# Expert layers of a two-layer trunk: unit 6's first half-weights loaded beside unit 4's, register reads per unit, gate products inside the second up product

## The chip, the cores and the metric

The kernel runs on one core of a Trainium2 chip. The metric is the device time of one execution in microseconds, the median of the runs. Times inside an execution are microseconds from the start of its span. Bytes are given as the profile gives them.

## What is computed

The program is a two-layer decoder trunk over 256 tokens of width 1024, float32 throughout. Layer 0 mixes with a state-space and a short-convolution mixer, layer 1 with two kinds of block-sparse attention. Each is followed by a hierarchical mixture of experts, which is what matters here:

```python
def hier_moe(h, w_group, b_group, w_expert, b_expert, w_gate, w_up, w_down):
    ...
    gi = jnp.argmax(gl, axis=-1)                                  # one of 4 groups per token
    ...
    ev, ei = lax.top_k(jax.nn.softmax(el, axis=-1), EXPERT_TOPK)  # 2 of the group's 4 experts
    ...
    h1 = jnp.einsum('td,edf->tef', xt, w_gate)
    h3 = jnp.einsum('td,edf->tef', xt, w_up)
    act = jax.nn.silu(h1) * h3 * gate[..., None].astype(h1.dtype)
    y = jnp.einsum('tef,efd->td', act, w_down)
```

There are 16 experts of 256 hidden units. Each has a gate, an up and a down matrix of 1 MB; a layer reads all 48 of them.

## The kernel before, in words

`moe(l, out_of)` computes one expert layer. Tokens are routed on the chip. `places` writes one-hot tables `Pm` that pick each expert's tokens; `gather(g, c0, c1)` multiplies the tokens by them and gives `xg`, the gathered tokens of a pair of units, in two halves of four column blocks. Work is done in seven units: units 0 to 5 have two experts with 64 token places each, unit 6 has four experts with 32 places each. Experts 0 to 5 stand fixed in units 0 to 2; `arrange` sorts the other ten by load, and their numbers (`ids`) are read into registers of SyncE, which issues all weight transfers in program order.

For unit j: `loads(j)` issues the gate and up weights, `downs(j)` the down weights, `up(j)` multiplies the gathered tokens by gate and up (c = 0..7 outside, the experts inside), `act(j)` applies SiLU on ScalarE and the product with the gate value `gs` on VectorE, `turn(j, a)` transposes the result on TensorE with a copy `aT` on VectorE, `down(j, f)` multiplies by half f of the down weights, `split` (L210 to L212) breaks the result into two parts on ScalarE and VectorE, and `scatter(j, f)` adds it back to `h` through the turned one-hot tables `PT`, which `ptrans(g)` makes.

Weights lie in slabs of 1 MB. Ten of them are a ring (`slab()`), and four more (`spare_slabs`) hold unit 2's gate and up weights and later the first halves of unit 6's. An expert's gate and up weights fill two slabs; `load_half(l, e, m, s)` issues the two transfers of one of them, for c = 4m to 4m + 3. A transfer into a slab waits until the work that reads its old content is done, and everything behind it in SyncE's queue waits too. In the loop, unit j's step issues the weights of unit j + 2 and the down weights of unit j + 1.

`gates` computes gate products: 14 small matmuls over the tables `Pm` and the gate values `Gs` (from `gate_values`, VectorE) whose sums give `gs` and the scale `rsl`, which `act` needs. The overflow test reads `nmax` into a register of every engine and branches around `overflow`, which is not taken here. PSUM tiles come from tags with a fixed number of buffers: `tp` has two, used by `gates`, `ptrans`, `gather` and `turn`; `mm` has two, used by `up`.

Each engine executes its instructions in the order in which the program issues them; the order is written out by hand.

Of the kernel before, what the change touches and what calls it, by code (L numbers as in the profile page):

```python
# [21 lines left out]
P = 128  # L22
# [38 lines left out]
FIX = 6  # L61
# [4 lines left out]
def tile_trunk(ctx: ExitStack, tc: tile.TileContext, x, cst, sml, s5c, ev_w_in, ev_w_out, od_w_in, od_w_out,  # L66
               cw1k, cw1v, w_gate, w_up, w_down, out):
    nc = tc.nc
# [7 lines left out]
    def ps(tag, shape, dt=F32):  # L76
        return psum.tile(shape, dt, name=tag, tag=tag, bufs={"acc": 3, "mm": 2, "tp": 2, "o": 1}[tag])
# [15 lines left out]
    def cs(n):  # L93
        o, w = _CST[n]
        return C[:, o:o + w]
# [12 lines left out]
    def slab():  # L108
        return ring.tile([P, 2048], F32, name="slab")
# [35 lines left out]
    def expert(w, l, e):  # L145
        return w[l, e] if isinstance(e, int) else w[l, bass.ds(e, 1)].rearrange("o a b -> (o a) b")

    def load_expert(l, e, s=None):

        return [load_half(l, e, m, slab() if s is None else s[m]) for m in range(2)]  # L150

    def load_half(l, e, m, s):
        v = s.rearrange("p (k c n) -> p k c n", k=2, c=4)
        for k, w in enumerate((w_gate, w_up)):
            sy.dma_start(v[:, k], expert(w, l, e).rearrange("(p c) f -> p c f", c=8)[:, 4 * m:4 * m + 4])  # L155
        return v

    def load_down(l, es):

        out = []  # L160
        for e in es:
            s = slab().rearrange("p (c n) -> p c n", c=2)
            sy.dma_start(s, expert(w_down, l, e).rearrange("(p c) d -> p c d", c=2))
            out.append(s)
        return out
# [1072 lines left out]
    def moe(l, out_of):  # L1238
        with tc.tile_pool(name=f"moe{l}", bufs=1, reuse_waits="tile") as sp:
# [39 lines left out]
            for t in range(2):  # L1279
                p = ps("tp", [P, 20])  # L1280
# [32 lines left out]
            nd = 16 - FIX  # L1313
            sd, ids, Q = T("sd", (P, 2, nd)), T("ids", (P, nd), I32), T("Q", (P, nd, nd))
            slx, nmax = T("slx", (P, 2, 16)), T("nmax", (P, 1), I32)

            def places(a, b):

                n, w = b - a, 64 if a < 12 else 32
                o = 64 * a if a < 12 else 768 + 32 * (a - 12)  # L1320
                for t in range(2):
                    v = sl[:, t, a:b] if a < FIX else sd[:, t, a - FIX:b - FIX]
                    tt(Pm[:, t, o:o + n * w].rearrange("p (e s) -> p e s", e=n), v[:, :, None].to_broadcast([P, n, w]),
                       cs("iota")[:, None, 0:w].to_broadcast([P, n, w]), op=OP.is_equal)
# [67 lines left out]

            def gates():

                p = ps("tp", [P, 512])
                for j in range(7):
                    for t in range(2):
                        pe.matmul(p[:, 34 * j:34 * j + 192], pair(t, j), Gs[:, t], start=(t == 0), stop=(t == 1))
                for k in range(2):
                    v = p[64 * k:64 * k + 64]  # L1400
                    d = bass.AP(tensor=v.tensor, offset=v.offset + k, ap=[v.ap[0], [36, 6], [16, 2]])
                    tr(gs[64 * k:64 * k + 64, 0:6, None], d, axis=AX.X, op=OP.add)
                for k in range(4):
                    v = p[32 * k:32 * k + 32]
                    d = bass.AP(tensor=v.tensor, offset=v.offset + 34 * 6 + 12 + k, ap=[v.ap[0], [1, 1], [16, 2]])
                    tr(gs[32 * k:32 * k + 32, 6:7, None], d, axis=AX.X, op=OP.add)
                d = bass.AP(tensor=p.tensor, offset=p.offset + 32, ap=[p.ap[0], [34, 7], [1, 2]])
                tr(rsl[:, :, None], d, axis=AX.X, op=OP.add)
                tt(gs, gs, rsl, op=OP.mult)
# [22 lines left out]
            def ptrans(g):  # L1432
                p = ps("tp", [P, 2, 2, P])
                n = 2 if g < 3 else 1
                for jj in range(n):
                    for t in range(2):
                        pe.transpose(p[:, jj, t], pair(t, 2 * g + jj).bitcast(F32), ident)  # L1437
                ac.activation(PT[:, 2 * g:2 * g + n], p[:, :n], AF.Copy)

            wgu, wd, pgu, ys = {}, {}, {}, {}  # L1440

            who = list(range(FIX))
            of = lambda j: who[2 * j:2 * j + 2] if j < 6 else who[12:]
            spare_slabs = lambda: [T(f"slab{i}", (P, 2048)) for i in range(4)]

            def loads(j):
                if j == 2:
                    x = spare_slabs()
                    wgu[j] = [load_expert(l, e, x[2 * k:2 * k + 2]) for k, e in enumerate(of(j))]
                elif j == 6:  # L1450

                    x = spare_slabs()
                    v = [load_half(l, e, m, x[k] if m == 0 else slab()) for m in range(2) for k, e in enumerate(of(j))]
                    wgu[j] = [[v[k], v[4 + k]] for k in range(4)]
                elif j < 7:
                    wgu[j] = [load_expert(l, e) for e in of(j)]

            def downs(j):
                wd[j] = load_down(l, of(j))

            def up(j):
                pgu[j] = p = ps("mm", [P, 2, 256])
                n = len(wgu[j])
                w = P // n
                for c in range(8):
                    for k in range(n):
                        o = P * (j % 2) + w * k
                        pe.matmul(p[w * k:w * k + w], xgs[j // 2][:, c, o:o + w], wgu[j][k][c // 4][:, :, c % 4],  # L1468
                                  start=(c == 0), stop=(c == 7), tile_position=(0, w * k))
# [51 lines left out]
            up(0)  # L1521
            arrange()
            gate_values()
            places(4, 6)
            places(6, 12)
            places(12, 16)
            gates()
            ptrans(0)
            cnt = nc.values_load(nmax[0:1, 0:1], min_val=0, max_val=288)
            with tc.If(cnt > 64):  # L1530
                overflow(sp, l, xT, slx, Gf, rs, T("xg", (P, 8, 256), bufs=2))
            a = act(0)
            for j in range(6):
                g = j // 2
                if j == 1:
                    who += [nc.values_load(ids[0:1, i:i + 1], engines=(mybir.EngineType.SP,), min_val=FIX, max_val=15)
                            for i in range(nd)]
                if j:
                    loads(j + 2)
                downs(j + 1)  # L1540
                up(j + 1)
                aT = turn(j, a)
                if j:
                    scatter(j - 1, 0)
                a = act(j + 1)
                more = j % 2 == 0
                if more:
                    gather(g + 1, 0, 4)
                down(j, 0)
                if j:  # L1550
                    scatter(j - 1, 1)
                down(j, 1)
                if more:
                    gather(g + 1, 4, 8)
                else:
                    ptrans(g + 1)
# [53 lines left out]
    moe(0, False)  # L1610
    odd()
    moe(1, True)


# [93 lines left out]
```

## Time and profile before

| | |
|---|---|
| median of 3 runs | 530.35 us (528.98 to 530.55) |
| the profiled execution | 529.48 us, its span 527.8 us |
| TensorE (PE) busy | 490.3 us, 93% |
| VectorE (DVE) busy | 293.4 us, 56% |
| ScalarE (ACT) busy | 212.9 us, 40% |
| transfers | 137.63 MB, mean 261 GB/s |

The first expert layer lies between about 119 and 247 us of the span, the second between about 395 and 524 us. Busy time is that of an engine's instructions; an engine that is busy for most of the span can still have short waits that set the end. A releaser (behind `<-`) is what ended an idle time.

### The profile page before, as it was taken

How to read it: one execution, taken by the hardware profiler on the slowest of the kernel's cores; microseconds unless marked ns; L12 is line 12 of the kernel's file. 1: busy time of each engine (PE TensorE's matmuls, PEld its weight loads, DVE VectorE, ACT ScalarE, POOL GpSimd, SP SyncE). 2: the span in 40 equal slices, each digit the busy share in tenths (PEclk: the TensorE clock that was granted, in tenths of full speed). 3: DMA queues.
4: the chain of work that ended last, by engine and by line, in shares of the span. 5: the costliest groups of instructions: out<-in, count | busy, mean ns of one | idle time of the engine just before them, and what ended most of it. 6: DMA issues, size and time to landing. Idle time of an engine off the chain costs nothing. (4 is left out here: it accounts for less than half of the span.)

```text
span 527.8 us, 9043 instructions
## 1 busy us (share of the span) xinstructions
PE 490.3 (93%) x3245; PEld 330.9 (63%) x3245; DVE 293.4 (56%) x682; ACT 212.9 (40%) x468; POOL 138.9 (26%) x292
## 2 busy tenths in 40 slices
PE   7998979998899999998899889989998899999995
PEld 5997979786354443544878778878785453443441
DVE  5876597656723323434654687977456623333432
ACT  4646623754131111214546777777563121111110
POOL 6899970001000000100355556651230000000000
PEclk9999997999999999999999999999999899999999
DMA  8949933357497899999959400440088595999992
GB/s 299 405 136 381 380 116 111 130 213 266 172 339 289 289 397 403 413 420 399 377 189 377 174 2 13 142 160 8 2 283 354 204 362 233 323 390 412 398 385 84
DMA packets 36591, 137.63 MB, mean 261 GB/s; under 512 B 4544, under 2 KB 8768, under 8 KB 31424
## 3 DMA queue, kind: packets, MB, share of 16 engines
q1 hardware_dynamic: 36544, 137.03, 68.5%
q8 instruction: 27, 0.44, 0.3%
q14 instruction: 20, 0.16, 0.1%
HBM read 135.70 MB, written 1.05 MB: 259 GB/s over the span
## 5 line engine op out<-in xcount | busy, mean ns | idle before, releaser
L1468 PE MATMUL mm<-slab,xg 128*64 128x512 f32 (+1 forms) x512 | 101.4, 595 | 1.6 <-DMA slab<-in_w_up_dram 1.0
L1468 PEld LDWEIGHTS mm<-slab,xg 128*64 128x64 f32 (+1 forms) x512 | 34.5, 130 | 58.3 <-issue 56.2
L1485 DVE COPY aT<-tp 128x256 f32<-128x256 f32 x14 | 6.0, 425 | 76.9 <-PE tp L1483 76.9
L212 DVE TENSOR_TENSOR w<-slab,w 128x1024 fp32r<-128x1024 f32 (+2 forms) x39 | 40.0, 1034 | 13.5 <-ACT w L211 12.3
L313 PE MATMUL mm<-xh,w 128*128 128x256 f32 x288 | 41.2, 293 | 3.8 <-DVE yb L372 3.3
L211 ACT ACTIVATE w<-slab 128x512 fp32r<-128x512 f32 (+2 forms) x57 | 43.3, 780 | 1.3 <-PE mm L837 0.9
L313 PEld LDWEIGHTS mm<-xh,w 128*128 128x128 f32 x288 | 38.1, 200 | 4.2 <-issue 4.2
L837 PE MATMUL mm<-w,xh 128*128 128x256 f32 x256 | 38.6, 293 | 0.2 <-ACT xh L242 0.2
L1474 ACT ACTIVATE si<-mm,rsl 128x256 f32<-128x256 f32 x14 | 6.7, 475 | 75.7 <-PE mm L1468 67.8
L837 PEld LDWEIGHTS mm<-w,xh 128*128 128x128 f32 x256 | 33.3, 189 | 1.2 <-ACT xh L242 0.9
L1497 PE MATMUL o<-slab,aT 128*64 128x512 f32 (+1 forms) x128 | 29.5, 604 | 2.9 <-DMA slab<-in_w_down_dram 2.9
L1509 DVE TENSOR_TENSOR h<-h,acc 128x512 f32<-128x512 f32 x44 | 28.2, 682 | 2.8 <-PE acc L1506 2.8
L212 DVE TENSOR_TENSOR ylp<-o,xlp 128x512 fp32r<-128x512 f32 x14 | 9.7, 692 | 34.4 <-ACT xlp L211 34.4
L1497 PE MATMUL acc<-slab,aT 128*64 128x512 f32 (+1 forms) x128 | 28.6, 600 | 0.0
L849 POOL MEMSET fl<- 128x2048 f32 x1 | 1.8, 1805 | 98.9 <-PE tp L1422 98.9
L212 POOL TENSOR_TENSOR w<-slab,w 128x512 fp32r<-128x512 f32 (+1 forms) x18 | 24.0, 1343 | 13.9 <-ACT w L211 9.5
L1428 ACT ACTIVATE xg<-tp,sml 128x256 f32<-128x256 f32 (+1 forms) x32 | 12.6, 444 | 36.0 <-PE tp L1422 36.0
L407 PE MATMUL acc<-w,yh 128*128 128x512 f32 x80 | 25.7, 400 | 0.0
L211 ACT ACTIVATE xlp<-o 128x512 fp32r<-128x512 f32 x14 | 8.4, 598 | 42.8 <-PE acc L1506 28.3
L1107 ACT ACTIVATE pr<-acc,mx 128x128 f32<-128x128 f32 (+1 forms) x56 | 22.9, 424 | 0.1
L398 DVE TENSOR_TENSOR w<-slab,w 128x512 fp32r<-128x512 f32 (+1 forms) x18 | 17.1, 963 | 10.4 <-ACT w L397 8.7
L1422 PEld LDWEIGHTS tp<-Pm,xhm 128*128 128x128 f32 x128 | 16.5, 189 | 9.7 <-issue 4.9
(436 smaller groups left out, 1004.0 us busy)
## 6 DMA issues: line engine op xcount, KB each, us to landing
slab<-in_w_gate_dram SPq DMA_DIRECT2D x64, 512.0 KB, 8.4
slab<-in_w_up_dram SPq DMA_DIRECT2D x64, 512.0 KB, 9.1
slab<-in_w_down_dram SPq DMA_DIRECT2D x32, 1024.0 KB, 10.4
slab<-in_ev_w_in_dram SPq DMA_DIRECT2D x8, 1024.0 KB, 13.9
slab<-in_od_w_in_dram SPq DMA_DIRECT2D x8, 1024.0 KB, 12.7
slab<-in_ev_w_out_dram SPq DMA_DIRECT2D x4, 1024.0 KB, 12.3
slab<-in_od_w_out_dram SPq DMA_DIRECT2D x4, 1024.0 KB, 8.8
slab<-in_ev_w_in_dram SPq DMA_DIRECT2D x4, 512.0 KB, 7.6
```

The costliest lines, as they stand in the source:

```text
L211: ac.activation(hi, src, AF.Copy)
L212: (eng or ve).tensor_tensor(lo, src, hi.bitcast(F32), op=OP.subtract)
L313: pe.matmul(p, a[:, c], b[:, c], start=(c == 0 and n == 0), stop=(c == 7 and n == 2))
L398: (po if s.done in s.pool else ve).tensor_tensor(wl, v[:, o:o + s.n], wh.bitcast(F32), op=OP.subtract)
L407: pe.matmul(acc[t, f], a[:, c, t * P:(t + 1) * P], b[:, f * 512:(f + 1) * 512], start=(first and m == 0), stop=(last and m == 2))
L837: pe.matmul(acc[i][t], a[:, c0 + k, t * P:(t + 1) * P], b[:, k], start=(c0 + k == 0 and m == 0 and (n > 256 or t == 0)), stop=(c0 + k == 7 ...
L1107: ac.activation(pr[:, q * nk:(q + 1) * nk], U[u]["s"][:, q * w:q * w + nk], AF.Exp, bias=U[u]["m"][:, q:q + 1], accum_out=su[:, q:q + 1])
L1422: pe.matmul(p[b][:, d], v[:, t, c], Pm[:, t, 256 * g:256 * g + n_], start=(n + d + t == 0), stop=(n + t == 2), skip_group_check=True)
L1428: ac.activation(xgs[g][:, c, :n_], p[b][:, d], AF.Copy, scale=w)
L1468: pe.matmul(p[w * k:w * k + w], xgs[j // 2][:, c, o:o + w], wgu[j][k][c // 4][:, :, c % 4], start=(c == 0), stop=(c == 7), tile_position=( ...
L1497: pe.matmul(py[v], aT[:, c, v], wd[j][k][:, c, f * 512:(f + 1) * 512], start=(c == 0), stop=(c == 1), tile_position=(0, w * k))
L1509: tt(v, v, q[t], op=OP.add)
```

## The change

In each expert layer, `up(1)` is cut into two halves and moved. Its first half (c = 0..3) now stands ahead of the gate products, its second half between `ptrans(0)` and the overflow test. `downs(1)` is issued ahead of the test. The first half of `gather(1)` moves ahead of `turn(0)`. `places(12, 16)` is called inside `gates`, at the same place in VectorE's order.

The register reads are no longer ten in a row: `of(j)` reads the registers of a unit when its weights are first asked for. The first halves of unit 6 (into the four spare slabs) are issued with unit 4, between the weights of its first and its second expert; unit 6's own step issues the second halves alone.

```diff
             def gates():
 
+                places(12, 16)
                 p = ps("tp", [P, 512])
...
-            who = list(range(FIX))
-            of = lambda j: who[2 * j:2 * j + 2] if j < 6 else who[12:]
+            who = {}
+
+            def of(j):
+
+                if j not in who:
+                    a, b = (2 * j, 2 * j + 2) if j < 6 else (12, 16)
+                    who[j] = [i if i < FIX else nc.values_load(ids[0:1, i - FIX:i - FIX + 1], min_val=FIX, max_val=15,
+                                                               engines=(mybir.EngineType.SP,)) for i in range(a, b)]
+                return who[j]
...
+                elif j == 4:
+
+                    wgu[j] = [load_expert(l, of(j)[0])]
+                    wgu[6] = [[load_half(l, e, 0, x)] for e, x in zip(of(6), spare_slabs())]
+                    wgu[j].append(load_expert(l, of(j)[1]))
                 elif j == 6:
-
-                    x = spare_slabs()
-                    v = [load_half(l, e, m, x[k] if m == 0 else slab()) for m in range(2) for k, e in enumerate(of(j))]
-                    wgu[j] = [[v[k], v[4 + k]] for k in range(4)]
+                    for k, e in enumerate(of(j)):
+                        wgu[j][k].append(load_half(l, e, 1, slab()))
...
-            def up(j):
-                pgu[j] = p = ps("mm", [P, 2, 256])
+            def up(j, c0=0, c1=8):
+                if c0 == 0:
+                    pgu[j] = ps("mm", [P, 2, 256])
+                p = pgu[j]
...
-                for c in range(8):
+                for c in range(c0, c1):
...
             gate_values()
+            up(1, 0, 4)
             places(4, 6)
             places(6, 12)
-            places(12, 16)
             gates()
             ptrans(0)
+            up(1, 4, 8)
+            downs(1)
             cnt = nc.values_load(nmax[0:1, 0:1], min_val=0, max_val=288)
...
             for j in range(6):
                 g = j // 2
-                if j == 1:
-                    who += [nc.values_load(ids[0:1, i:i + 1], engines=(mybir.EngineType.SP,), min_val=FIX, max_val=15)
-                            for i in range(nd)]
+                more = j % 2 == 0
                 if j:
                     loads(j + 2)
-                downs(j + 1)
-                up(j + 1)
+                    downs(j + 1)
+                    up(j + 1)
+                else:
+                    gather(1, 0, 4)
                 aT = turn(j, a)
...
-                more = j % 2 == 0
-                if more:
+                if j and more:
                     gather(g + 1, 0, 4)
```

TensorE's order from unit 0's up product (L1468 before, L1482 now) to unit 0's down product (L1497 before, L1511 now), the rows of the branch's untaken side left out. Before:

```order
L1468 MATMUL mm<-slab,xg 64x512 x16
L1398 MATMUL tp<-Gs,Pm 128x192 x14
L1437 MATMUL tp<-sml,Pm 128x128 x4
L1529 TENSOR_LOAD nmax
L1530 COMPARE_AND_BRANCH
...
L1468 MATMUL mm<-slab,xg 64x512 x16
L1483 MATMUL tp<-sml,act 128x128 x2
L1422 MATMUL tp<-Pm,xhm 128x256 x8
L1422 MATMUL tp<-Pm,xlm 128x256 x8
L1497 MATMUL o<-slab,aT 64x512 x4
```

Now:

```order
L1482 MATMUL mm<-slab,xg 64x512 x24
L1399 MATMUL tp<-Gs,Pm 128x192 x14
L1438 MATMUL tp<-sml,Pm 128x128 x4
L1482 MATMUL mm<-slab,xg 64x512 x8
L1545 TENSOR_LOAD nmax
L1546 COMPARE_AND_BRANCH
...
L1423 MATMUL tp<-Pm,xhm 128x256 x8
L1423 MATMUL tp<-Pm,xlm 128x256 x8
L1497 MATMUL tp<-sml,act 128x128 x2
L1511 MATMUL o<-slab,aT 64x512 x4
```

Eight of unit 1's sixteen up matmuls have moved ahead of the gate products and eight ahead of the branch, and the gather's first half stands ahead of the turn, not behind it.

SyncE's queue at unit 4 of layer 0; `slab_2110` to `slab_2113` are the four spare slabs, and in the ring's rows gate and up alternate. Before, unit 4's four slabs were followed by unit 3's down weights:

```order
L155 DMA slab<-in_w_gate_dram 128x1024
L155 ISA
L155 DMA slab<-in_w_up_dram 128x1024
L163 ISA
L163 DMA slab<-in_w_down_dram 128x2048
L163 ISA
L163 DMA slab<-in_w_down_dram 128x2048
```

Now, behind unit 4's first expert:

```order
L155 DMA slab<-in_w_up_dram 128x1024
L1449 TENSOR_LOAD ids
...
L155 DMA slab_2110<-in_w_gate_dram 128x1024
L155 ISA
L155 DMA slab_2110<-in_w_up_dram 128x1024
...
L155 DMA slab_2113<-in_w_gate_dram 128x1024
L155 ISA
L155 DMA slab_2113<-in_w_up_dram 128x1024
L155 ISA
L155 DMA slab<-in_w_gate_dram 128x1024
```

Four register reads and eight transfers of unit 6 now stand between unit 4's first and second expert.

## Rows read from the trace of the kernel before

**Rows 1.** The page: the span, and TensorE's busy time, share of the span and instructions.
```profile
span 527.8 us, 9043 instructions
PE 490.3 (93%) x3245; PEld 330.9 (63%) x3245; DVE 293.4 (56%) x682; ACT 212.9 (40%) x468; POOL 138.9 (26%) x292
```
**Rows 2.** The chain of work that ended last, in order of time: start, duration, what.
```profile
474.46 13.91 DMA slab<-in_w_up_dram
...
499.00 17.87 DMA slab<-in_w_down_dram
```
**Rows 3.** TensorE's timeline in layer 0, from unit 0's second gather half and up product to the start of unit 2's up product: start, duration, engine, line, operation, count, idle time before it and its releaser.
```profile
129.14 1.25 PE L1422 MATMUL tp<-Pm,xhm 128*128 128x256 f32 x8 [0.69 <-ACT xg L1428]
...
131.26 7.09 PE L1468 MATMUL mm<-slab,xg 128*64 128x512 f32 x32
140.47 2.37 PE L1398 MATMUL tp<-Gs,Pm 128*128 128x192 f32 x14 [2.13 <-DVE Gs L1388]
142.68 0.60 PE L1437 MATMUL tp<-sml,Pm 128*128 128x128 f32 x4
143.57 7.18 PE L1468 MATMUL mm<-slab,xg 128*64 128x512 f32 x32 [0.30 <-PEq L1530]
150.68 0.44 PE L1483 MATMUL tp<-sml,act 128*128 128x128 f32 x2
...
151.64 0.98 PE L1422 MATMUL tp<-Pm,xhm 128*128 128x256 f32 x6 [0.28 <-DVE aT L1485]
...
153.46 1.94 PE L1497 MATMUL o<-slab,aT 128*64 128x512 f32 x8
...
157.04 1.21 PE L1422 MATMUL tp<-Pm,xhm 128*128 128x256 f32 x8
...
159.12 7.09 PE L1468 MATMUL mm<-slab,xg 128*64 128x512 f32 x32
```
**Rows 4.** TensorE's timeline in layer 1: units 0 and 2's up products, the gate products, and the two waits in unit 6.
```profile
406.53 7.09 PE L1468 MATMUL mm<-slab,xg 128*64 128x512 f32 x32
415.74 3.15 PE L1398 MATMUL tp<-Gs,Pm 128*128 128x192 f32 x14 [2.12 <-DVE Gs L1388]
...
435.50 7.09 PE L1468 MATMUL mm<-slab,xg 128*64 128x512 f32 x32
...
502.14 3.59 PE L1468 MATMUL mm<-slab,xg 128*32 128x512 f32 x26 [0.69 <-DMA slab<-in_w_up_dram]
...
516.92 1.47 PE L1497 MATMUL o<-slab,aT 128*32 128x512 f32 x9 [1.43 <-DMA slab<-in_w_down_dram]
```
**Rows 5.** TensorE's timeline in layer 0: unit 3's up product and the turn behind it, unit 4's up product, and the two waits in unit 6.
```profile
172.88 7.09 PE L1468 MATMUL mm<-slab,xg 128*64 128x512 f32 x32
179.90 0.44 PE L1483 MATMUL tp<-sml,act 128*128 128x128 f32 x2
...
189.95 7.09 PE L1468 MATMUL mm<-slab,xg 128*64 128x512 f32 x32
...
225.36 3.59 PE L1468 MATMUL mm<-slab,xg 128*32 128x512 f32 x26 [0.31 <-DMA slab<-in_w_up_dram]
...
240.20 1.48 PE L1497 MATMUL o<-slab,aT 128*32 128x512 f32 x9 [1.44 <-DMA slab<-in_w_down_dram]
```
**Rows 6.** The timeline of SyncE's queue (SPq) in layer 0: the last transfer for unit 4's first expert, the first for its second, and the first for unit 6.
```profile
158.81 0.33 SPq L155 DMA_DIRECT2D slab<-in_w_up_dram  x1
172.38 0.33 SPq L155 DMA_DIRECT2D slab<-in_w_gate_dram  x1
...
194.73 0.33 SPq L155 DMA_DIRECT2D slab<-in_w_gate_dram  x1
```
**Rows 7.** Stretches of 5 us in layer 0: the stretch, its length, the engines' busy time and instructions, the granted clock, the share of the transfer engines, GB/s.
```profile
165.00:170.00 5.00, 5.00 (x23) 2.09 (x20) 2.11 (x4) 0.48 (x1) 0.00 (x0) 1.00 0.52 210
170.00:175.00 5.00, 5.00 (x25) 1.73 (x25) 2.57 (x4) 1.75 (x3) 0.00 (x0) 1.00 0.30 93
175.00:180.00 5.00, 5.00 (x25) 1.54 (x22) 0.00 (x0) 0.00 (x0) 0.00 (x0) 1.00 0.91 265
180.00:185.00 5.00, 5.00 (x31) 3.32 (x31) 2.98 (x6) 1.32 (x3) 0.00 (x0) 1.00 1.03 430
```
**Rows 8.** VectorE's timeline in layer 0: the last one-hot tables, and unit 0's activation.
```profile
140.74 1.42 DVE L1323 TENSOR_TENSOR Pm<-sd,cst 128x384 fp32r<-128x384 f32 x4
...
147.24 0.48 DVE L1476 SCALAR_TENSOR_TENSOR act<-mm,gs,si 128x256 f32<-128x256 f32 x1 [2.95 <-ACT si L1474]
```
**Rows 9.** ScalarE's timeline in layer 0: the table load ahead of unit 0's SiLU, and the two copies of one gather half.
```profile
145.44 1.28 ACT L1474 ACT_TABLE_LOAD   x1 [1.47 <-DVEq L1530]
...
153.34 0.84 ACT L1428 ACTIVATE xg<-tp,sml 128x256 f32<-128x256 f32 x2 [2.02 <-PE tp L1422]
```
**Rows 10.** The stretches of the gate products of layers 0 and 1, columns as in Rows 7.
```profile
140.50:143.00 2.50, 2.39 (x17) 2.09 (x18) 1.78 (x7) 0.00 (x0) 0.00 (x0) 1.00 1.01 423
415.00:420.00 5.00, 3.96 (x19) 3.60 (x19) 3.34 (x17) 0.28 (x1) 0.00 (x0) 0.66 0.68 281
```
**Rows 11.** The instructions of L1536, the register reads of both layers: duration in ns least, median, greatest, and the first and last start.
```profile
L1536 SPq TENSOR_LOAD <-ids x20: 261/267/282, 137.6 to 418.1; - x20
L1536 SPq FUSED_REGOPS  x20: 147/147/154, 137.9 to 418.4; - x20
```
**Rows 12.** The transfers of L163, the down weights, issued between 190 and 246 us.
```profile
DMA to landing us min/median/max: 8.0/13.1/17.0
```

## Prediction

> **What bounds the kernel now.** I read the page's totals first, then the chain of waits, then TensorE's timeline through both expert layers, and last the queue that issues the weight transfers. TensorE is busy for 93% of the span [rows 1], so a change pays only where it fills one of TensorE's waits or shortens its work. The chain that ended last [rows 2] runs from 474 us to 517 us almost wholly through weight transfers and only then back into matmuls: in the second expert layer the weights of the last units arrive too late.
>
> TensorE's timeline shows four kinds of wait in each expert layer. (a) Between the first up product and the gate products TensorE idles 2.13 us in layer 0 [rows 3] and 2.12 us in layer 1 [rows 4]: VectorE is still computing the gate values Gs. (b) After the overflow branch it idles 0.30 us, and after the first turn it idles until VectorE has copied aT; from the start of that turn to the next matmul behind the copy it is 151.64 - 150.68 = 0.96 us [rows 3]. (c) In unit 6's up product it waits for a second half of weights, 0.31 us [rows 5] and 0.69 us [rows 4]. (d) In unit 6's down product it waits 1.44 us [rows 5] and 1.43 us [rows 4].
>
> The cause of (c) and (d) stands in the transfer queue. After 158.81 us it issues nothing until 172.38 us: the next transfer goes into a slab that unit 1's down product still reads [rows 6]. The rate falls to 210, 93 and 265 GB/s in the three stretches from 165 to 180 us, and then runs at 430 [rows 7]. From 194.73 us [rows 6] unit 6's eight slabs and the last six down slabs are wanted at once, and unit 6 pays for the hole.
>
> **The change, part by part.** Layer 0 is worked out from the start of unit 0's up product to the start of unit 2's, which takes 159.12 - 131.26 = 27.86 us now [rows 3]. An unhindered up product of two experts takes 179.90 - 172.88 = 7.02 us from its start to the next work [rows 5], half of one 3.51. The new order costs, step by step:
>
> - up(0), 7.02: to 138.28.
> - first half of up(1), 3.51: to 141.79. Its weights were issued long before and its gathered tokens are the ones that up(0) reads, so it has nothing to wait for.
> - gate products. Gs is complete before VectorE starts its last one-hot tables at 140.74, and these end at 142.16 [rows 8]. So the wait of 2.13 is gone. The products cost 142.68 - 140.47 = 2.21 now [rows 3]; some of this may be waiting for the tables, but I keep all of it: to 144.00.
> - the turned one-hot tables, 0.60 [rows 3]: to 144.60.
> - second half of up(1), 3.51: to 148.11.
> - the branch. I take the 0.30 that it costs today [rows 3], since the engine still drains ahead of it: to 148.41.
> - first half of gather(1), 159.12 - 157.04 = 2.08 [rows 3]: to 150.49.
> - a new wait. The turn now needs a PSUM buffer that the gather's copies must first empty. The nearest row is the second gather half of unit 0's pair, which stands in the same position behind the first half, 0.69 [rows 3]: to 151.18. Bounds: nothing, and 0.84 more if both of ScalarE's copies come after the last matmul (they are two of the kind that took 0.84 together [rows 9]).
> - the turn with the wait for its copy, 0.96 as now [rows 3], which no gather work covers any more: to 152.14.
> - both halves of down(0), 157.04 - 153.46 = 3.58 [rows 3]: to 155.72.
> - second half of gather(1), 2.08: to 157.80.
>
> So unit 2 starts at 157.80 and not at 159.12: **1.3 us** in layer 0. Of the 2.13 us filled, 0.8 go back into the turn's two waits, since the gather that covered them has moved ahead.
>
> In layer 1 the same stretch takes 435.50 - 406.53 = 28.97 us [rows 4], 1.11 more than in layer 0. The work is the same; the granted clock was 0.66 in the stretch of its gate products, and 1.00 in layer 0's [rows 10], that is, part of it ran at 1.2 GHz instead of 2.4. The engine had waited 2.12 us just before. With matmuls in the place of that wait I expect the full clock, so the gain there is 1.3 + 1.1 = **2.4 us**. The Trainium skill, "TensorE: Matmul & The Clock Gate", Part 1, says that the array's clock is halved by inactivity and released by sustained activity; by that the 1.1 us go with the wait. The trace agrees in layer 1 and not in layer 0, where the same wait left the clock at 1.00.
>
> **The transfers.** The first halves of unit 6 go into the four spare slabs, which up(2) frees, half of them at its middle and the rest by its end, some 166 us [rows 3, 5]. They are four slabs of 1024 KB, 4.2 MB. The hole in [rows 7] has room for (410 - 210 + 410 - 93 + 410 - 265) GB/s x 5 us = 3.3 MB, with 410 GB/s for a full queue, a little under the 430 shown. So the work behind it comes 3.3 MB / 410 GB/s = 8 us earlier at the least. Unit 6's late slabs were 0.31 and 1.44 us late, and TensorE will ask 1.3 us earlier: 8 us covers 1.44 + 1.3 = 2.7. Both waits go: 0.31 + 1.44 = **1.75 us** in layer 0, 0.69 + 1.43 = **2.12 us** in layer 1. Bounds: nothing, and these sums. I take them whole, because the margin is 5 us.
>
> **What else moves, at nothing.** Ten register reads take their place one by one: each is a load of 0.27 and a register operation of 0.15 us [rows 11], some 0.5 with the gaps. Now only two stand ahead of unit 3's first weights, which therefore start some 4 us earlier; unit 3 does not wait for weights today, so this buys nothing by itself. The four reads of unit 6's registers, 2 us, fall into the queue's 13 us of waiting. Unit 1's down slabs are issued ahead of the branch, which only the transfer queue sees. The branch itself is passed later by TensorE alone. The chain from the gate products to the turn has to be watched: from the start of the turned tables at 142.68 to the end of unit 0's activation at 147.24 + 0.48 = 147.72 it is 5.04 us [rows 3, 8], with ScalarE's table load of 1.28 in it [rows 9]. From 144.00 this gives 149.04, and the turn asks at 151.18: 2.1 us in hand.
>
> **The sum.** 1.3 + 2.4 + 1.75 + 2.12 = 7.6 us. The profiled execution took 529.48 us, so 521.9; it stands 0.87 us below the median of 530.35, from which the same sum gives 522.8. I give **522.4**, between them. The stretches between the expert layers are bound by TensorE's order, and their weights come earlier too, so I let the gain of layer 0 pass through whole. About 0.3%, 1.6 us, is what a measurement here can tell from no change.
>
> **Rivals.**
> 1. The clock falls in both layers. Three waits of 0.3, 0.69 and about 0.5 us now stand within four microseconds. For it: layer 1 [rows 10]; against it: waits like these stand around gather(0) in layer 0 at a clock of 1.00. It costs the 1.11 us of layer 1 twice: 522.4 + 2.2 = 524.6. The Trainium skill, same page, "A second HAM failure mode", says that frequent short idling between groups of matmuls makes the clock swing; that speaks against this change, and by it this rival is the outcome.
> 2. The cover is too thin: unit 0's activation comes later than the turn by more than the 2.1 us in hand and the 1.3 us gained per layer are lost: 522.4 + 2.6 = 525.0. Against it: every link of the 5.04 us is a row, and none has the changed work in it.
> 3. The transfers do not gain: unit 6's first halves come early, but the down slabs, issued last, stay late. Then only 3.7 us remain: 526.3. For it: the queue is full from 180 us on [rows 7] and the down slabs need up to 17.0 us to land [rows 12]. Against it: 4.2 MB less stand ahead of them.
> 4. Slower: unit 4's second expert is now issued behind unit 6's first halves. It would be issued at 172.38 - 1.3 = 171 us [rows 6] and is wanted at 189.95 - 1.3 = 188.7 [rows 5]. If it lands later than 17.6 us after issue, every further microsecond delays TensorE, in both layers; from 22.4 us on (2 x 4.8 = 9.6 more) the kernel is slower than before. The longest landing shown is 17.0 [rows 12]; at 23 us it costs 2 x 5.4 = 10.8, and the time is 533. The Trainium skill, "DMA: Bandwidth & Descriptors", "Queues, rings and completion order", says that each transfer engine takes its descriptors in ring order, so that what is issued first is ahead; by it the eight early transfers stand ahead, as this rival has it, and no row shows the order on an engine. Against the rival: the hole nearly holds the 4.2 MB, and the 0.9 left over are 2 us.
> 5. No change that can be measured, because something in the layers between takes the gain back: about 530.
>
> **How the numbers follow.** The forecast has 0.72; rival 1 has 0.09, rival 2 0.06, rival 3 0.08, rival 4 0.02, rival 5 0.03. The forecast's own range is 520.2 (no new wait at the turn, 2 x 0.69 less, and 0.8 for half of the spread of the three runs) to 524.0 (0.84 more at the turn in one layer, and the same 0.8). With rivals 1 and 2 the range is 520.2 to 525.2, which leaves out 0.13. Faster by over 0.3%: forecast and rivals 1 to 3, 0.95; within 0.3%: 0.03; slower: 0.02.
>
> **What would show it.** In the changed profile: no idle time of TensorE ahead of the gate products; about 0.7 ahead of unit 0's turn and 0.5 ahead of unit 0's down product; the granted clock 1.00 through layer 1's gate products; some 26.5 us from up(0) to up(2) in both layers; no wait for a weight transfer in unit 6; a transfer rate above 380 GB/s from 160 to 180 us. A wait for weights ahead of unit 4's up product, or unit 6's waits unchanged, would prove me wrong.

## The result, and the profile after

The changed kernel takes 516.39 us (median of 4 runs, 514.40 to 516.89) against 530.45 us (median of 4, 528.98 to 531.46): a ratio of 0.9739, 95% interval 0.9714 to 0.9765. It is 14.1 us faster. The forecast was 522.4 us with a range from 520.2, so the time lies below the range. The direction and the places were right; the size was not.

The profiled execution after took 516.22 us with a span of 514.6, against 529.48 and 527.8 before. Its page:

```profile
span 514.6 us, 9047 instructions
PE 483.6 (94%) x3245; PEld 324.7 (63%) x3245; DVE 293.4 (57%) x682; ACT 212.7 (41%) x468; POOL 138.4 (27%) x292
```

TensorE has the same 3245 instructions as in [rows 1] and a span 13.2 us shorter. Its timeline in layer 0 from unit 0's up product to the start of unit 2's, which answers to [rows 3] (start, duration, engine, line, operation, count, idle time before it and its releaser):

```profile
131.11 10.52 PE L1482 MATMUL mm<-slab,xg 128*64 128x512 f32 x48
141.56 1.81 PE L1399 MATMUL tp<-Gs,Pm 128*128 128x192 f32 x14
143.21 0.60 PE L1438 MATMUL tp<-sml,Pm 128*128 128x128 f32 x4
143.74 3.65 PE L1482 MATMUL mm<-slab,xg 128*64 128x512 f32 x16
147.73 1.19 PE L1423 MATMUL tp<-Pm,xhm 128*128 128x256 f32 x8 [0.34 <-PEq L1546]
...
150.53 0.44 PE L1497 MATMUL tp<-sml,act 128*128 128x128 f32 x2 [0.70 <-ACT xg L1429]
151.48 1.94 PE L1511 MATMUL o<-slab,aT 128*64 128x512 f32 x8 [0.52 <-DVE aT L1499]
...
157.15 7.09 PE L1482 MATMUL mm<-slab,xg 128*64 128x512 f32 x32
```

The wait of 2.13 us ahead of the gate products is gone. The three waits that were forecast stand where they were forecast: 0.34 behind the branch, 0.70 ahead of the turn, 0.52 ahead of the down product. The stretch takes 157.15 - 131.11 = 26.04 us instead of 27.86. Layer 1, which answers to [rows 4], now takes the same, 426.56 - 400.55 = 26.01 instead of 28.97:

```profile
400.55 10.52 PE L1482 MATMUL mm<-slab,xg 128*64 128x512 f32 x48
...
426.56 7.09 PE L1482 MATMUL mm<-slab,xg 128*64 128x512 f32 x32
```

Unit 6 is read best from stretches: from the start of its up product to the turn behind it, and from the start of its down product to the scatter behind it, in layer 0 and then layer 1. The columns are the stretch, its length, the busy time and instructions of PE, PEld, DVE, ACT and POOL, the granted clock, the share of the transfer engines and GB/s. Before:

```profile
220.56:228.88 8.32, 8.01 (x65) 2.21 (x65) 0.61 (x2) 0.51 (x2) 1.80 (x1) 1.00 1.03 419
237.53:243.75 6.22, 4.78 (x33) 1.17 (x32) 0.69 (x1) 0.60 (x1) 0.00 (x0) 1.00 1.02 423
496.96:505.67 8.71, 8.02 (x66) 2.22 (x65) 0.61 (x2) 0.51 (x2) 0.00 (x0) 1.00 1.01 417
514.35:520.47 6.12, 4.69 (x33) 1.13 (x33) 0.69 (x1) 0.60 (x1) 0.00 (x0) 1.00 0.04 15
```

After:

```profile
218.59:225.59 7.00, 7.00 (x65) 1.97 (x64) 0.61 (x2) 0.51 (x2) 1.80 (x1) 1.00 1.01 413
234.21:237.78 3.57, 3.57 (x33) 0.94 (x32) 0.69 (x1) 0.60 (x1) 0.00 (x0) 1.00 0.98 400
488.01:495.02 7.01, 7.01 (x66) 1.98 (x65) 0.61 (x2) 0.51 (x2) 0.00 (x0) 1.00 1.00 420
503.62:507.19 3.57, 3.57 (x33) 0.94 (x32) 0.69 (x1) 0.60 (x1) 0.00 (x0) 1.00 0.00 0
```

The same matmuls are PE's whole occupation now, and the four stretches are shorter by 1.32, 2.65, 1.70 and 2.55 us, 8.2 in all. The idle times printed in [rows 4, 5] add up to 0.31 + 1.44 + 0.69 + 1.43 = 3.87. That difference is what the experiments had to explain.

The sum of the stages, by differences of starts in the two timelines:

| stage | before | after | gained | forecast |
|---|---|---|---|---|
| layer 0, up(0) to up(2) | 27.86 | 26.04 | 1.82 | 1.3 |
| layer 1, up(0) to up(2) | 28.97 | 26.01 | 2.96 | 2.4 |
| layer 0, unit 6's two stretches | 8.32 + 6.22 | 7.00 + 3.57 | 3.97 | 1.75 |
| layer 1, unit 6's two stretches | 8.71 + 6.12 | 7.01 + 3.57 | 4.25 | 2.12 |
| sum | | | 13.0 | 7.6 |

The other 0.2 us of the span lie almost wholly ahead of layer 0's up(0), which starts at 131.11 instead of 131.26. Between the last scatter of layer 0 and up(0) of layer 1 it is 162.78 before and 162.77 after: the gain passes through whole. The medians differ by 0.8 us more than the profiled executions (14.06 against 13.26), since that of before stood 0.97 below its median and that of after 0.17.

The issues of SyncE's queue behind unit 4's first expert, which answer to [rows 6], are the first of unit 6's halves and the first of unit 4's second expert:

```profile
160.83 0.33 SPq L155 DMA_DIRECT2D slab<-in_w_gate_dram  x1
...
170.41 0.33 SPq L155 DMA_DIRECT2D slab<-in_w_gate_dram  x1
```

The transfer rates of the stretches of [rows 7] are, columns as above:

```profile
165.00:170.00 5.00, 5.00 (x23) 1.74 (x21) 3.02 (x7) 0.60 (x1) 0.00 (x0) 1.00 0.93 321
170.00:175.00 5.00, 5.00 (x26) 1.91 (x26) 1.30 (x3) 1.15 (x2) 0.00 (x0) 1.00 0.98 322
175.00:180.00 5.00, 5.00 (x28) 2.63 (x25) 1.33 (x3) 0.48 (x1) 0.00 (x0) 1.00 1.02 417
```

So 210, 93 and 265 GB/s became 321, 322 and 417; that is 2.5 MB more in these 15 us. The chain that ended last has no transfer in it any more. In [rows 2] it ran through weight transfers from 474 us on; now it reads there (start, duration, what):

```profile
471.25 7.02 PE mm L1482 x32
...
505.55 1.76 PE acc L1511 x16
```

### The profile page after: what moved, and what is told of

The parts are those of the page before. It is cut to its first block, busy times and chain, and to the rows that moved or that the text cites. A ratio compares the mean times of both kernels' runs of the same rounds, so it can differ in the third digit from the quotient of the medians.

```text
span 514.6 us, 9047 instructions
## 1 busy us (share of the span) xinstructions
PE 483.6 (94%) x3245; PEld 324.7 (63%) x3245; DVE 293.4 (57%) x682; ACT 212.7 (41%) x468; POOL 138.4 (27%) x292
## 5 line engine op out<-in xcount | busy, mean ns | idle before, releaser
L1482 PE MATMUL mm<-slab,xg 128*64 128x512 f32 (+1 forms) x512 | 99.2, 595 | 0.0
L1482 PEld LDWEIGHTS mm<-slab,xg 128*64 128x64 f32 (+1 forms) x512 | 30.5, 130 | 58.3 <-issue 55.4
L1511 PE MATMUL o<-slab,aT 128*64 128x512 f32 (+1 forms) x128 | 27.1, 603 | 1.0 <-DVE aT L1499 1.0
L1511 PE MATMUL acc<-slab,aT 128*64 128x512 f32 (+1 forms) x128 | 26.9, 600 | 0.0
```

What stands on the lines that cost most here:

```text
L1511: pe.matmul(py[v], aT[:, c, v], wd[j][k][:, c, f * 512:(f + 1) * 512], start=(c == 0), stop=(c == 1), tile_position=(0, w * k))
```

## The experiments

The theory was that the two halves of the change, the new order and the early halves, add up, and that a late weight slab in unit 6 costs TensorE more than the idle time in its row. "Front" is the stretch of a layer from the start of up(0) to the start of up(2). Each comparison is with the kernel before on the same chip. That median was 530.83 us (13 runs) for the first four and 529.64 us (17 runs) for the other four.

**The new order alone.** The change with the reads and unit 6's loads as before.

```diff
-            who = {}
...
+            who = list(range(FIX))
+            of = lambda j: who[2 * j:2 * j + 2] if j < 6 else who[12:]
...
-                elif j == 4:
-
-                    wgu[j] = [load_expert(l, of(j)[0])]
-                    wgu[6] = [[load_half(l, e, 0, x)] for e, x in zip(of(6), spare_slabs())]
-                    wgu[j].append(load_expert(l, of(j)[1]))
```

> The kernel before with the new order of TensorE's work alone (up(1) in two halves around the gate products, downs(1) ahead of the branch, gather(1) ahead of the turn); ten register reads in a row and unit 6's weights in unit 6's step, as before. My theory: the front of each layer gets shorter by what the changed kernel shows, 1.82 us in layer 0 and 2.96 in layer 1 from up(0) to up(2), and since the slab that ends the hole in the transfer queue is freed as much earlier, unit 6's weights come earlier by as much and its stretches keep their 8.32 and 6.22 us: some 4.8 us faster than before, 525.6. Rival: the weights of unit 6 land when they did, so the front's gain is spent waiting there: 529 to 530.

Measured: 524.07 us (522.27 to 525.58, 4 runs), ratio 0.9874, 0.9829 to 0.9919. The fronts of both layers took 26.04 and 26.05 us. Unit 6 in layer 0, on TensorE's timeline:

```profile
217.74 8.13 PE L1471 MATMUL mm<-slab,xg 128*32 128x512 f32 x64
...
234.46 1.18 PE L1500 MATMUL o<-slab,aT 128*32 128x512 f32 x6
237.08 1.48 PE L1500 MATMUL o<-slab,aT 128*32 128x512 f32 x9 [1.44 <-DMA slab<-in_w_down_dram]
...
240.63 0.73 PE L1509 MATMUL acc<-xlp,PT 128*128 128x512 f32 x2
```

The down product's stretch is 240.63 - 234.46 = 6.17 us, as late as before: the earlier arrival of TensorE was not eaten by a longer wait for weights. And the up product shows no idle time in its row at all, yet its stretch takes 8.06 us, about 1 more than the 7.00 after the change. The single records show the wait: from 221.20 on only three of the four experts' matmuls start together, twice, and all four again at 222.28, 0.65 us behind the last three instead of 0.43. A wait can be there without any idle time printed.

**The early halves alone.** Before, with the loads of units 4 and 6 of the change.

```diff
-                elif j == 6:
+                elif j == 4:
...
+                    wgu[j] = [load_expert(l, of(j)[0])]
+                    wgu[6] = [[load_half(l, e, 0, x)] for e, x in zip(of(6), spare_slabs())]
+                    wgu[j].append(load_expert(l, of(j)[1]))
+                elif j == 6:
+                    for k, e in enumerate(of(j)):
+                        wgu[j][k].append(load_half(l, e, 1, slab()))
```

> The kernel before with unit 6's first half-weights issued between unit 4's two experts, and nothing else of the change. My theory: unit 6's waits cost what its stretches show over the changed kernel's, 8.32 - 7.00 and 6.22 - 3.57 in layer 0 and 8.71 - 7.01 and 6.12 - 3.57 in layer 1, 8.2 us in all, not the 3.87 us that the idle times of the rows add up to: 522.2. Rival (the idle times shown are all that the waits cost, the rest of the gain is from the earlier register reads or the new order): 526.5.

Measured: 522.86 us (521.81 to 523.08, 4 runs), ratio 0.9849, 0.9812 to 0.9886. Unit 6 in layer 0:

```profile
219.47 7.07 PE L1471 MATMUL mm<-slab,xg 128*32 128x512 f32 x64
...
235.09 1.92 PE L1500 MATMUL o<-slab,aT 128*32 128x512 f32 x16
...
238.66 0.73 PE L1509 MATMUL acc<-xlp,PT 128*128 128x512 f32 x2
```

Both stretches are down to 7.00 and 3.57, in layer 1 as well. The early halves alone bring 8.0 us of the median (6 to 10 by the interval) where the forecast gave them 3.87, and the four stretches got 8.2 shorter. In the two profiled executions the gain is 6.4 us: layer 1's front took 30.37 us, 1.4 more than before, and the way from layer 0's last scatter to layer 1's up(0) 164.35 instead of 162.78, both with falls of the clock, while layer 0's up(0) came 1.1 us earlier. With the 6.8 us of the order alone the medians make 14.7; the whole change brought 14.1. Within their intervals the parts add up.

**The register reads alone.** Before, with `of(j)` reading the registers of a unit when they are asked for.

```diff
-            who = list(range(FIX))
+            who = {}
+            def of(j):
+                if j not in who:
...
-                if j == 1:
-                    who += [nc.values_load(ids[0:1, i:i + 1], engines=(mybir.EngineType.SP,), min_val=FIX, max_val=15)
```

> The kernel before with the register reads per unit alone. My theory: unit 3's first weights start some 4 us earlier, which nobody waits for, and from unit 1's down product on the queue is as before: 530.4, no change. Rival (the ten reads hold back the queue, and unit 6's late weights are late by it): up to 4 us faster, 526.

Measured: 529.82 us (527.62 to 532.24, 10 runs), ratio 0.9983, 0.9959 to 1.0006: no difference that shows. Its profiled execution (531.89 us) is worth a look for another reason. TensorE in layer 0, and the stretches around the gate products of layers 0 and 1:

```profile
138.98 3.15 PE L1398 MATMUL tp<-Gs,Pm 128*128 128x192 f32 x14 [2.14 <-DVE Gs L1388]
...
143.29 8.90 PE L1476 MATMUL mm<-slab,xg 128*64 128x512 f32 x32 [0.30 <-PEq L1538]
```
```profile
139.00:144.00 5.00, 4.61 (x20) 3.59 (x22) 2.97 (x14) 0.60 (x1) 0.00 (x0) 0.61 0.99 352
414.00:419.00 5.00, 2.87 (x13) 2.45 (x12) 3.90 (x17) 0.00 (x0) 0.00 (x0) 0.75 0.96 399
```

Behind the same wait of 2.1 us the granted clock was 0.61 and 0.75 of full speed, a mixture of 1.2 and 2.4 GHz, in both layers. The unhindered 32 matmuls of up(1) took 8.90 us instead of 7.18 [rows 3]. The fronts were 30.82 us in layer 0 and 30.30 in layer 1, against 27.86 with the clock at 1.00. So the kernel before carried a cost that varied from execution to execution.

**The change without the early halves.** The order and the reads of the change, unit 6's loads as before.

```diff
-                elif j == 4:
-
-                    wgu[j] = [load_expert(l, of(j)[0])]
-                    wgu[6] = [[load_half(l, e, 0, x)] for e, x in zip(of(6), spare_slabs())]
-                    wgu[j].append(load_expert(l, of(j)[1]))
...
+                    x = spare_slabs()
+                    v = [load_half(l, e, m, x[k] if m == 0 else slab()) for m in range(2) for k, e in enumerate(of(j))]
+                    wgu[j] = [[v[k], v[4 + k]] for k in range(4)]
```

> The changed kernel with unit 6's weights all issued in unit 6's step, as before; order and register reads as changed. My theory: unit 6's stretches are as long as before the change, 8.2 us more than in the changed kernel: 516.4 + 8.2 = 524.6, and with the first experiment within 1 us of it. Rival (the waits cost the idle times that the rows show): 520.3.

Measured: 523.65 us (523.17 to 524.16, 4 runs), ratio 0.9874, 0.9838 to 0.9910, the same as the order alone. Fronts of 26.01 and 26.02 us, unit 6's stretches 8.01 and 6.18 in layer 0. Its gain of 7.2 us is more than the 1.82 + 2.96 = 4.8 of the two fronts in the pair of profiled executions. About 1 us comes from unit 6's up product (8.32 to 8.01 and 8.71 to 7.97). The rest, 1.3 us, was not followed to its place. An estimate: in the four profiles that keep the wait as it was (before, the early halves alone, the reads alone and unit 6 with weights that are there) the eight fronts lie 0 to 3.0 us above 27.86, 1.3 on the mean, so 2.6 per execution; the profile of before has 1.11 of that, which leaves 1.5 for a median to gain more than this pair shows.

**The turn inside the gather.** The change, with unit 0's turn put between the two parts of the gather's first half, in a PSUM buffer of another tag, so that it need not wait for the gather's copies.

```diff
-            def gather(g, c0, c1):
+            def gather(g, c0, c1, between=None):
...
+                    if between and n == 1 and t == 0:
+                        between()
...
-                    gather(1, 0, 4)
-                aT = turn(j, a)
+                    early = []
+                    gather(1, 0, 4, lambda: early.append(turn(0, a, "acc")))
+                aT = turn(j, a) if j else early[0]
```

> The changed kernel with unit 0's turn moved into the first half of gather(1), between its products with the high and with the low parts, and given a PSUM buffer of another tag (acc). Then the turn waits for no copy of the gather (0.70 us now), and the eight products behind it cover the copy aT (0.52 us). My theory: the stretch from up(0) to up(2) falls from 26.04 to 24.8 us in both layers, 2.4 us in all: 514.0. Rival: unit 0's activation, complete at 148.25 in layer 0, or VectorE's copies that now come after aT, take the place of the waits: no change, 516.4.

Measured: 512.33 us (512.05 to 512.75, 6 runs), ratio 0.9675, 0.9651 to 0.9699, faster than both kernels (the change had 0.9714 to 0.9765). TensorE in layer 0:

```profile
146.80 1.19 PE L1425 MATMUL tp<-Pm,xhm 128*128 128x256 f32 x8 [0.34 <-PEq L1548]
147.83 0.38 PE L1499 MATMUL acc<-sml,act 128*128 128x128 f32 x2
147.96 1.19 PE L1425 MATMUL tp<-Pm,xlm 128*128 128x256 f32 x8
149.08 1.94 PE L1513 MATMUL o<-slab,aT 128*64 128x512 f32 x8
```

Two of the change's three new waits, 0.70 and 0.52 us, are gone: unit 0's activation is there although the turn comes 1.8 us earlier, counted from up(0) (17.65 us behind it instead of 19.42), and the second part of the gather covers the copy aT. The front is 24.56 us in both layers instead of 26.04. That makes 2 x 1.48 = 3.0 of the 4.0 us by which its span of 510.6 is under that of the change; another 0.93 lies ahead of up(0), where the programs are alike and the clock fell otherwise (0.79 from 78 to 86 us, against 0.57 in the profile of the change), so it is not this edit's.

**One expert of unit 6 cut short.** Of the fourth expert's products in unit 6 only the first up and the first down product are left.

```diff
+                        if k == 3 and c:
+                            continue
```

The same two lines stand in `up` and in `down`; the sums of the fourth expert are then incomplete.

> The changed kernel in which unit 6's fourth expert computes only the first of its eight up products and the first of its two down products. My theory: the four experts' matmuls run beside one another, each in its 32 columns of the array, at one step of 0.43 us for all four, so leaving out most of one expert shortens nothing: unit 6's stretches stay 7.0 and 3.57 us, and in the trace three matmuls start together where four did. By the same a late expert, which catches up alone, costs its lag over again. Rival (the matmuls share the array's time one after another): seven of 32 and four of 16 are missing, 1.5 and 0.9 us less per layer, 511.6.

The whole time, 1055.95 us, says nothing on this question: layer 1 routed its tokens by the altered values and took the overflow branch. Layer 0's unit 6 lies ahead of that and can be read:

```profile
217.54 7.07 PE L1484 MATMUL mm<-slab,xg 128*32 128x512 f32 x50
224.53 0.44 PE L1499 MATMUL tp<-sml,act 128*128 128x128 f32 x2
...
233.14 1.49 PE L1515 MATMUL o<-slab,aT 128*32 128x512 f32 x11
...
236.70 0.74 PE L1524 MATMUL acc<-xlp,PT 128*128 128x512 f32 x2
```

With 50 instead of 64 records the up product still takes 224.53 - 217.54 = 7.0 us, and the down product 3.56. The four experts' matmuls run side by side, each in its 32 columns, one step for all four, and leaving most of one out saves nothing. The 64 records are 16 steps, so one is 7.0 / 16 = 0.44 us. The Trainium skill, "TensorEngine Tiling (Array Packing)", "Key Properties", says that different tiles of the array can execute matmuls in parallel; this run agrees.

**Unit 6 with weights that are there.** Before, with unit 6 multiplying by other weights that have long landed: the first half for both halves of the up product, unit 5's down weights for its own. Unit 6's results are then other ones, so layer 1 routes its tokens by altered values.

```diff
-wgu[j][k][c // 4][:, :, c % 4],
+wgu[j][k][0 if n == 4 else c // 4][:, :, c % 4],
...
-wd[j][k][:, c, f * 512:(f + 1) * 512],
+(wd[5][k % 2] if n == 4 else wd[j][k])[:, c, f * 512:(f + 1) * 512],
```

> The kernel before in which unit 6 reads weights that are there: its first halves in place of the second, and unit 5's down weights in place of its own. All transfers are issued as before; only the reading of the late ones is left out. My theory: the stretches of unit 6 fall to 7.0 and 3.57 us in both layers, from 8.0 to 8.7 and 6.2, which is 8 us: 522.5. Rival (the waits cost the idle times that the rows show, 3.87 us): 526.8.

Measured: 524.45 us (522.79 to 525.00, 4 runs), ratio 0.9899, 0.9863 to 0.9934: 2 us more than expected. Unit 6's stretches took exactly 7.00 and 3.57 in both layers, so all 8.2 us there hang on late weights. Part of the gain was lost elsewhere in the profiled execution. A fall of the clock made layer 0's front 29.29 us, 1.4 more than before, while layer 1's had none (27.86, 1.1 less). From layer 0's last scatter to layer 1's up(0) it took 164.38 us instead of 162.78, with the granted clock at 0.73 from 310 to 316 us, where before had 1.00. And TensorE now reached unit 5's down product before its weights, in layer 0:

```profile
229.56 1.07 PE L1497 MATMUL o<-slab,aT 128*64 128x512 f32 x2
230.81 1.93 PE L1497 MATMUL o<-slab,aT 128*64 128x512 f32 x6 [0.18 <-DMA slab<-in_w_down_dram]
```

The row says 0.18 us of idle. From unit 6's turn to its down product, where this lies, it was 9.85 us instead of 8.65 before: 1.2 us lost, again several times the idle time printed, here with two experts side by side. In layer 1 it was 0.2. Ahead of layer 0's up(0) 0.7 us were won. So 8.2 - 1.4 + 1.1 - 1.6 - 1.2 - 0.2 + 0.7 = 5.6 us, which is the difference of the two spans, 527.8 - 522.2.

**The wait filled.** Before, with nine matmuls on zeros ahead of the gate products.

```diff
+            warm(9)
             gates()
```

> The kernel before with nine idle matmuls (on zeros, as its own warm-up does) in the place of the wait ahead of the gate products; no work is moved. My theory: the wait itself stays, since the gate values come when they come, but the granted clock stays at 2.4 GHz behind it, so the stretch from up(0) to up(2) is 27.9 us in both layers in every run, where profiles without the filling had 27.86 to 30.82: some 1.5 us per layer on the mean, 527.8. Rival (the clock's falls behind the wait are chance or come from elsewhere): 530.8, with falls in the profile.

Measured: 527.69 us (525.91 to 530.16, 12 runs), ratio 0.9959, 0.9937 to 0.9982. TensorE in layer 0:

```profile
137.56 2.12 PE L251 MATMUL tp<-zero 128*128 128x512 bf16 x9
139.75 2.37 PE L1398 MATMUL tp<-Gs,Pm 128*128 128x192 f32 x14
```

The fronts were 27.85 us in both layers, and the granted clock 1.00 around the gate products of both. That is one profiled execution; of the others only the mean clock of the whole span is known, 0.993 over the 12 runs against 0.988 over the 17 of before. No work was saved; only the engine was kept busy. So the clock's falls behind this wait cost the kernel before about 2 us of its median (1.0 to 3.3 by the interval). The Trainium skill, "TensorE: Matmul & The Clock Gate", Part 1, has inactivity as what halves the clock; the run agrees, with 1.00 behind the filled wait.

## Why the prediction was wrong, point by point

**The step that failed** is the term for unit 6: "Both waits go: 0.31 + 1.44 = 1.75 us in layer 0, 0.69 + 1.43 = 2.12 us in layer 1", with the bound "nothing, and these sums". That both waits go was right, and no unit 6 row waits for a transfer now. The term was mis-sized: 3.87 us were forecast, 8.2 measured, 4.4 of the 5.4 us by which the stages gained more than foretold. I took the idle time in a row for the price of the wait. No rival stood on the fast side either, so the range ended at 520.2. What the rows around it show, before, in layer 0:

```profile
220.56 4.49 PE L1468 MATMUL mm<-slab,xg 128*32 128x512 f32 x38
...
237.53 1.24 PE L1497 MATMUL o<-slab,aT 128*32 128x512 f32 x6
...
241.51 0.59 PE L1497 MATMUL o<-slab,aT 128*32 128x512 f32 x1
241.52 2.30 PE L1497 MATMUL acc<-slab,aT 128*32 128x512 f32 x13
243.75 0.73 PE L1506 MATMUL acc<-xlp,PT 128*128 128x512 f32 x2
```

An undisturbed up product has 4 matmuls in each of its 16 steps. Here 38 = 8 x 4 + 2 x 3 ran before the wait: eight full steps, then two in which one expert's slab was missing and the other three went ahead. Only then did all four stand still, and only that last piece was printed as 0.31. Two steps are the two records of one product: in the program's order, c outside and the experts inside, the late expert's product of c = 4 stands behind the other three's of the same c and ahead of all of c = 5, so there was nothing else that the engine could take. When the slab came, the late expert had 8 steps left and the others 6 (8 + 3 x 6 = 26, [rows 5]). The engine worked 8 more steps: 228.88 - 225.36 = 3.52 us, 0.44 each. The two steps in which three went ahead were run over again by the late one alone. So the loss is the whole lateness of the slab: due at 220.56 + 8 x 0.43 = 224.0, in use at 225.36, 1.3 us, which is what the stretch lost. In the down product one expert's first step was due at 237.5 and ran from 240.20, 2.7 us late (6 = 2 x 3 ran before it); the printed 1.44 begins after the other experts had gone up to two steps ahead, and counts from modelled ends of records that last 0.59 where a step takes 0.43. The stretch lost 2.65. The lone matmul of the first half (o) at 241.51 is the late expert's, while the others are already in the second half (acc).

The bound could have been found beforehand. Unit 6's up product has 16 steps like that of two experts, which takes 7.02 us unhindered by the prediction's own rows [rows 5]; its 8.32 and 8.71 stand beside that in the same timeline.

**The second error** is the gate products, kept at 2.21 us with the remark that some of it may be waiting for the tables. 0.56 of it was: they take 143.21 - 141.56 = 1.65 now, and 1.65 in the order alone, while the filled wait, which leaves them where they stood, keeps them at 2.20. VectorE's last tables ended at 142.16 [rows 8], 1.7 us after the products' start at 140.47; after the change they end at 142.01, 0.45 after the start at 141.56:

```profile
140.59 1.42 DVE L1323 TENSOR_TENSOR Pm<-sd,cst 128x384 fp32r<-128x384 f32 x4
```

Before, two of the 14 products start at 141.35 and 141.81, each 0.05 us behind the end of a table; that makes 0.48 of the 0.56. It explains the rest of the gap, 0.5 in each layer's front; the other steps of the new order came out within 0.2 us each: 10.45 for up(0) and half of up(1) (10.53 forecast), 3.99 for the second half with the branch (3.81), 2.80 for gather and wait (2.77), 0.95 for turn and copy (0.96), 3.58 for down(0) (3.58).

**The clock.** The 1.11 us of layer 1 were forecast to go with the wait, and went. The stretch around its gate products:

```profile
411.00:416.00 5.00, 5.00 (x34) 3.06 (x34) 1.75 (x11) 1.46 (x2) 0.00 (x0) 1.00 0.98 304
```

1.00 stands where [rows 10] had 0.66. That a wait of 2.1 us lowers the clock in some executions and not in others, up to 3 us in one layer, the two layers of one profile could not tell; the runs with the wait left in showed it. In the four profiles that keep the wait as it was, the clock fell behind it in five of the eight fronts; in the eight fronts of four profiles with the new order (the change, the order alone, the change without the early halves, the turn inside), and in the two with the wait filled, in none. The clock falls in other places too, with the change as without it: 0.57 from 78 to 86 us in the profiles of before and after, 0.72 or 0.73 from 310 to 316 us in three of the experiments. So not all of the spread from run to run hangs on this wait.

**The rivals.** 1: the clock does not fall behind the three short waits. The stretches from the first of them to unit 2's up product, in layer 0 and layer 1:

```profile
147.00:157.00 10.00, 8.45 (x52) 5.12 (x50) 3.56 (x7) 3.12 (x7) 0.00 (x0) 1.00 1.03 419
417.00:427.00 10.00, 8.62 (x52) 5.32 (x54) 3.89 (x8) 2.96 (x7) 0.00 (x0) 1.00 1.03 415
```

It is 1.00 in both, so the rule of the Trainium skill, "TensorE: Matmul & The Clock Gate", "A second HAM failure mode", that frequent short idling makes the clock swing, is not borne out for waits of 0.34, 0.70 and 0.52 us. 2: unit 0's activation is ready in time. Its row on VectorE, start and duration first:

```profile
147.77 0.48 DVE L1490 SCALAR_TENSOR_TENSOR act<-mm,gs,si 128x256 f32<-128x256 f32 x1 [2.95 <-ACT si L1488]
```

It is complete at 148.25, 2.3 us before the turn at 150.53; 2.1 were forecast, and the turn inside the gather used 1.8 of it. 3: the down slabs come in time, in both layers. 4: unit 4's second expert is issued at 170.41 (171 was forecast), and no matmul waits for it. 5: the layers between keep 162.77 us. The register reads are worth nothing, as forecast. One sign missed: the rate from 165 to 175 us is 321 GB/s and not above 380, and 364 over the whole stretch from 160 to 180 us. The hole was filled by 2.5 MB and not by the 3.3 that I counted on, though the transfer engines were busy for 0.93 to 1.02 of the time, and the margin of 5 us bore it.

## What to carry to other kernels

Size a wait by the length of its stage, start to start, against the same stage where nothing hinders it (another unit, the other layer, the count of its steps); where several lanes share an engine, the idle time in the row is only what is left after the others have done what the program's order puts ahead of the late product. If a wait for VectorE stands between two products whose weights are there, put half of the second product into it: that filled it here and kept the clock. A freed buffer is worth a transfer at once, even one that is needed four units later, if the queue would otherwise stand still; the same hole shows again as late weights at the end.

## What the runs showed of the hardware beyond expectation

Four matmul streams in 32 columns each run as one step of 0.44 us for all four, and a stream with most of its matmuls left out saves nothing (7.0 us with 50 or 64 records). When one stream's weights were late, the others went ahead by the two steps that program order put before it and then stopped, and afterwards the late one alone set the end: 1.3 us of a slab's lateness showed as 0.31 of idle, 2.65 as 1.44, 1.2 as 0.18 with two streams, about 1 as nothing at all. Behind an unchanged wait of 2.1 us the granted clock was 1.00 in one execution and 0.61 in another; it fell in five of eight such places.
